# Decoder layer with two token mixers: gate projections by a scheme of seven block products on three of eight weight units, the two branch products moved behind them

## The chip, the core and the metric

The kernel runs on one core of a Trainium2 chip. The metric is the device time of one execution in microseconds (us). Five engines work side by side, each on a queue of its own that it takes in order: TensorE (PE; its weight loads are shown as PEld), VectorE (DVE), ScalarE (ACT), GpSimd (POOL) and SyncE (SP). SP issues the weight transfers from HBM; POOL issues the small transfers inside the layer. An engine that waits for a semaphore holds everything that stands behind it on its own queue.

## The reference, cut to what matters

256 tokens, width 2048, everything in fp32:

```
h = rmsnorm(x);  proj = h @ w_in        # q_a, c_kv, k_rope, z_mla, c_in, b_gate, c_gate, z_conv, g_mla, g_conv
attn  = causal_attention(...) * silu(z_mla);            y_mla  = attn @ w_o_mla
conv  = b_gate * conv3(c_gate * c_in) * silu(z_conv);   y_conv = conv @ w_o_conv
merged = sigmoid(g_mla) * y_mla + sigmoid(g_conv) * y_conv
out = x + rmsnorm(merged @ w_out)
```

The change touches `g_mla` and `g_conv` (two products of 256 x 2048 tokens with 2048 x 2048 weights), `y_mla`, `y_conv` and the order of the four.

## The kernel before

Every fp32 operand is held as two float32r parts: hi (rounded) and lo (the rest, source minus hi). A product of two operands is three matmuls, hi x hi, hi x lo and lo x hi (`product`). Weights come in units of 128 x 2048 fp32 (1 MB): SP loads a unit into one of three `raw` buffers, ACT writes hi (`whi`, L237) and DVE writes lo (`wlo`, L238), in halves of 1024 columns with five half buffers each. `take(i)` asks for unit i, keeps three loads ahead and splits one unit ahead. A plain unit holds four K rows of blocks: 4 K blocks x 2 token tiles x 3 = 24 matmuls of 128 x 512.

The order of the work is written out; PE keeps it. A first part makes the low-rank products, z, attention by heads and four convolution products per column block (`cv`, 16 x 4 units). A column block of the convolution is drained from PSUM by `channels_done` (L695 on ACT, L697 on ACT, L700 on DVE); the two PSUM banks `cv` are then free for the next one. `taps` and `channels_join` finish the convolution; `turned` (L312 to L323) transposes a tile on DVE into a buffer (`via`, `cw` or `mv`), sends it in four POOL transfers to DRAM (`far`) and brings it back in one.

The second part (`tokens`, PSUM tiles `sq`) goes over four blocks c of 512 output columns, and in each over n = g_mla, g_conv, y_mla, y_conv: four units each, 64 units and 1536 matmuls. The two gates read the tokens in `x_both` (hi and lo, 16 K blocks), the branches read `at_both` and `cv_both`, which ACT and DVE split from `at_f` and `cv_f` while the first gates run. A gate's PSUM goes through a sigmoid on ACT into a small buffer (L897); the branch sums are multiplied in on DVE (L907, L912, L913). The merged block is turned and split into `m_both` while the next block's products run. The third part (`out`) multiplies `m_both` by w_out in 16 units and normalises.

Pools are stacked: a pool opened after another has closed takes its memory, so its first writer waits for all readers of what lay there. The large pool `bp` holds the buffers of the first part, among them `cw` and `mv`, from which the last convolution tiles leave by POOL transfers.

Of the kernel before, what the change touches and what calls it, by code (L numbers as in the profile page):

```python
# [23 lines left out]
H = 16  # L24
# [13 lines left out]
UNIT = 2048  # L38
LINE = 32
HALF = UNIT // 2  # L40
SQ = S // 4
XW = S + R


PV = {}
# [34 lines left out]


@with_exitstack
def tile_layer(ctx: ExitStack, tc: tile.TileContext, xw, x, pos, pvec, post_g, wc, wz, wcv, wkr, wqk, wqr, wv, cwr, wsq, out):
    nc = tc.nc

    def matmul(*a, **kw):
# [9 lines left out]
    part = top.tile([P, LINE], F32, name="part")[:, :NT]  # L96
# [3 lines left out]
    wpool = ctx.enter_context(tc.tile_pool(name="wpool", bufs=1))  # L100
# [4 lines left out]

    plan = []

    def add(ap, width=UNIT):
        plan.append((ap, width))
        return len(plan) - 1  # L110


# [8 lines left out]
    for h in range(H):  # L121
        g, second = divmod(h, HG)
# [3 lines left out]
    order = []  # L126
# [11 lines left out]
        else:  # L138
            u_head[i][j] = add(wcv[i, j])

    u_d = [[[add(wsq[n, c, k]) for k in range(4)] for n in range(4)] for c in range(4)]
# [3 lines left out]
    u_out = {ck: add(wsq[4, ck[0], ck[1]]) for ck in out_order}  # L145

    raws, splits, early = {}, {}, {}
    done = {"raw": 0, "split": 0}

    def load_raw(i):  # L150
        ap, w = plan[i]
        t = early.get(i)
        if t is None:
            t = wpool.tile([P, UNIT], F32, name=f"raw{i}", tag="raw", bufs=3)
        cuts = {0: (S, XW, 2 * XW), 1: (0, XW, 2 * XW), 2: (0, XW, 2 * XW)}.get(i, (0, w))
        for a, b in zip(cuts[:-1], cuts[1:]):
            nc.sync.dma_start(out=t[:, a:b], in_=ap[:, a:b])
        raws[i] = t
        if i == u_ckv[1]:
            tc.keep_in_program_order(nc.sync.dma_start(out=x_tok, in_=x))  # L160

    def split_unit(i):
        t, w = raws.pop(i), plan[i][1]
        parts = []
        if i == u_kr:
            t = t[:, :w].rearrange("p (k c) -> p k c", k=KD)
            for h in range(2):
                both = wpool.tile([P, HALF], F32R, name=f"whi{i}_{h}", tag="whi", bufs=5)
                both = both[:, :].rearrange("p (k j c) -> p k j c", k=KD // 2, j=2)
                ks = slice(h * KD // 2, (h + 1) * KD // 2)  # L170
                split_act(both[:, :, 0], both[:, :, 1], t[:, ks])
                parts.append(both.rearrange("p k j c -> p k (j c)"))
            splits[i] = parts
            return
        if i <= u_qa[-1]:

            hi, lo = (wpool.tile([P, HALF], F32R, name=f"{o}{i}", tag=o, bufs=5) for o in ("whi", "wlo"))
# [5 lines left out]
            splits[i] = [(hi, lo)]  # L183
            return
        for h in range(0, w, HALF):
            n = min(HALF, w - h)
            if u_out[3, 0] <= i < u_out[3, 3]:
                hi, lo = (op.tile([P, HALF], F32R, name=f"w{o}{i}_{h}") for o in ("hi", "lo"))
            else:
                hi = wpool.tile([P, HALF], F32R, name=f"whi{i}_{h}", tag="whi", bufs=5)  # L190
                lo = wpool.tile([P, HALF], F32R, name=f"wlo{i}_{h}", tag="wlo", bufs=5)
            split_act(hi[:, :n], lo[:, :n], t[:, h : h + n])
            parts.append((hi, lo))
        splits[i] = parts

    def ahead(i, raw=3, split=1):
        while done["raw"] < min(i + raw, len(plan)):
# [9 lines left out]
    def take(i):  # L207
        ahead(i)
        parts = splits.pop(i)

        def piece(j, n):
            o = j * n
            h, o = o // HALF, o % HALF
            return parts[h][0][:, o : o + n], parts[h][1][:, o : o + n]

        return piece

# [18 lines left out]
    def split_act(hi, lo, src, keep=False):  # L236
        a = nc.scalar.activation(hi, src, AF.Copy)  # L237
        b = nc.vector.tensor_tensor(lo, src, hi.bitcast(F32), op=ALU.subtract)  # L238
        if keep:

            tc.keep_in_program_order(a)
            tc.keep_in_program_order(b)
# [30 lines left out]


    main = ctx.enter_context(ExitStack())
    hp = main.enter_context(tc.tile_pool(name="hp", bufs=1))
# [562 lines left out]


    bstack.close()
    cp = main.enter_context(tc.tile_pool(name="cp", bufs=1))
    at_both = cp.tile([P, H, 2 * S], F32R, name="at_both")
    cv_both = cp.tile([P, KD, 2 * S], F32R, name="cv_both")
    dp = main.enter_context(tc.tile_pool(name="dp", bufs=1))

    def split_turned(src, both, c, t):
        ks, ts = slice(4 * c, 4 * c + 4), slice(t * P, (t + 1) * P)
        lo = slice(t * P + S, (t + 1) * P + S)
        split_act(quarters(both[:, ks, ts]), quarters(both[:, ks, lo]), by_rows(src, 4), True)  # L850

    def split_branch(i):

        for t in range(NT):
            split_turned(at_t[:, i, t, :], at_both, i, t)

    def split_channels(i):

        j, t = divmod(i, NT)
        split_turned(cv_t[:, j, t, :], cv_both, j, t)  # L860

    def tokens(c, n, cols):

        pss = [bank(f"sq{c}_{n}_{t}") for t in range(NT)]
        for kk in range(4):
            w = take(u_d[c][n][kk])
            if c == 0 and n == 0:
                split_branch(kk)
            if c == 0 and n in (1, 2):
                split_channels(4 * (n - 1) + kk)  # L870
# [7 lines left out]
    def wide(name, t, bufs=1):  # L878
        return dp.tile([P, 512], F32, name=f"{name}{t}", tag=f"{name}{t}", bufs=bufs)

    def features(c, m, m_both):

        for t in range(NT):
            split_turned(m[t][:, :], m_both, c, t)

    waiting = m_both = None
    for c in range(4):
        gates = []
        for n in range(2):
            pss = tokens(c, n, x_both)  # L890
            if waiting is not None:
                features(c - 1, waiting, m_both)
                waiting = None
            sg = []
            for t in range(NT):
                g = wide(f"sg{n}_", t)
                nc.scalar.activation(g[:, :], pss[t][:, :], AF.Sigmoid, scale=r_col[:, t : t + 1])  # L897
                sg.append(g)
            gates.append(sg)
        m = gates[0]  # L900
        pss = tokens(c, 2, at_both)
        if c == 0:
            fstack.close()
            merged_pool = ctx.enter_context(tc.tile_pool(name="merged_pool", bufs=1, side="right"))
            m_both = merged_pool.tile([P, KD, 2 * S], F32R, name="m_both")
        for t in range(NT):
            nc.vector.tensor_tensor(m[t][:, :], pss[t][:, :], m[t][:, :], op=ALU.mult)  # L907
        pss = tokens(c, 3, cv_both)
        steps = []
        for t in range(NT):  # L910
            y = gates[1][t]
            nc.vector.tensor_tensor(y[:, :], pss[t][:, :], y[:, :], op=ALU.mult)  # L912
            nc.vector.tensor_tensor(m[t][:, :], m[t][:, :], y[:, :], op=ALU.add)  # L913
            steps.append(turned(m[t][:, :], y[:, :], 4))
        for go, _ in steps:
            go()
        for t, (_, come) in enumerate(steps):
            come(m[t][:, :])
# [36 lines left out]
    last = []  # L955
# [33 lines left out]
        finish(t, out_block(3, t, pss[t]))  # L989


def _cols(w):

    k, n = w.shape
    return np.ascontiguousarray(
        w.reshape(k // P, P, n // P, P).transpose(2, 1, 0, 3)
    ).reshape(n // P, P, k)


def _feat(v):  # L1000
# [79 lines left out]
```

## Time and profile before

| | |
|---|---|
| median of three runs | 1045.03 us (1044.26 to 1047.25) |
| span of the profiled execution, first to last instruction | 1045.6 us |
| second part (`sq`), on PE | starts at 602.63, ends at 950.83 |
| third part (`out`), on PE | ends at 1037.88 |

The span of the profiled execution lies inside the range of the three runs, 0.6 us above their median. A row of the timeline gives the start, the time, the engine, the line, what is written and read, how many instructions, and in brackets how long the engine was idle before it and what ended that. A row of the groups gives the count, the busy time, the mean of one in ns, and the idle time before.

### The profile page before, as it was taken

To read this page: it belongs to the slowest core of one execution; us is meant where nothing else is said; L and a number is where in the kernel's file an instruction comes from. 1 tells how busy PE (TensorE), PEld (TensorE's weight loads), DVE (VectorE), ACT (ScalarE), POOL (GpSimd) and SP (SyncE) were. 2 spreads that over 40 slices of the span, in tenths; PEclk is the share of its full clock that TensorE was granted. 3 is DMA by queue.
4 is the path that set the end of the run, shared out by engine and by line. 5 is a ranking of instruction groups with operands and counts; after the bars stand their busy time and mean duration, and the time that the engine had idled before them with its cause. 6 is when DMAs were issued, how large, how long until landed. Compare 5 with 4: busy or idle time off the path is not lost.

```text
span 1045.6 us, 12715 instructions
## 1 busy us (share of the span) xinstructions
PE 1029.9 (98%) x4694; PEld 857.5 (82%) x4694; DVE 684.0 (65%) x954; ACT 529.5 (51%) x731; POOL 179.7 (17%) x345
## 2 busy tenths in 40 slices
PE   9999999999999999999999999999999999999997
PEld 8888887888878878788888888888888888888885
DVE  7578778686787667777777776555564456445562
ACT  7766556555455455554555455434444434443451
POOL 7611221204111132212222220020010002002000
PEclk9999999999999999999999999999999999999999
DMA  8755766658665685757676865575566556558642
GB/s 344 297 187 189 255 206 207 223 200 306 186 228 214 199 288 174 266 195 243 210 254 218 277 208 201 201 242 189 181 211 225 201 191 223 195 197 318 236 171 81
DMA packets 41951, 231.04 MB, mean 221 GB/s; under 512 B 7520, under 2 KB 8224, under 8 KB 18976
## 3 DMA queue, kind: packets, MB, share of 16 engines
q1 hardware_dynamic: 29808, 197.54, 53.6%
q0 software_dynamic: 11648, 29.38, 8.5%
q10 hardware_dynamic: 432, 3.29, 0.8%
q8 instruction: 37, 0.61, 0.2%
q14 instruction: 26, 0.21, 0.1%
HBM read 214.48 MB, written 11.53 MB: 216 GB/s over the span
## 4 chain that ended last, share of the span: by engine, by line
PE 88%; DMA 4%; DVE 4%; issue 2%; ACT 1%; POOL 1%; DVEq 0%; POOLq 0%; ACTq 0%
PE sq L88 33%; PE cv L88 26%; PE out L88 8%; PE z L88 7%; DMA cw<-cwr_dram 2%; PE qa L88 2%; PE ckv L88 2%; PE vv L88 2%; PE kn L88 2%; PE qn L88 2%; DVE wlo L238 1%; PE sc L88 1%; DMA far<-via 1%; PE o L88 1%; DMA p<-far 1%
## 5 line engine op out<-in xcount | busy, mean ns | idle before, releaser
L238 DVE TENSOR_TENSOR wlo<-raw,whi 128x1024 fp32r<-128x1024 f32 (+1 forms) x370 | 441.8, 1198 | 295.3 <-ACT whi L237 284.8
L237 ACT ACTIVATE whi<-raw 128x1024 fp32r<-128x1024 f32 (+1 forms) x372 | 382.8, 1035 | 413.9 <-PE sq L88 181.1
L88 PE MATMUL cv<-whi,x_both 128*128 128x512 f32 x1024 | 324.6, 391 | 6.5 <-DVE cv_w L700 4.5
L88 PEld LDWEIGHTS cv<-whi,x_both 128*128 128x128 f32 x1024 | 193.0, 189 | 47.0 <-DVE cv_w L700 5.1
L88 PE MATMUL cv<-wlo,x_both 128*128 128x512 f32 x512 | 200.3, 391 | 0.0
L88 PE MATMUL sq<-whi,x_both 128*128 128x512 f32 x512 | 158.4, 389 | 0.0
L88 PEld LDWEIGHTS sq<-whi,x_both 128*128 128x128 f32 x512 | 96.1, 188 | 20.0
L88 PEld LDWEIGHTS cv<-wlo,x_both 128*128 128x128 f32 x512 | 96.6, 189 | 18.9
L88 PE MATMUL sq<-wlo,x_both 128*128 128x512 f32 x256 | 99.6, 389 | 0.0
L88 PE MATMUL z<-whi,x_both 128*128 128x512 f32 x256 | 80.6, 390 | 0.0
L88 PE MATMUL sq<-whi,at_both 128*128 128x512 f32 x256 | 79.5, 389 | 0.0
L88 PE MATMUL sq<-whi,cv_both 128*128 128x512 f32 x256 | 79.5, 389 | 0.0
L88 PE MATMUL out<-whi,m_both 128*128 128x512 f32 x256 | 78.9, 389 | 0.0
L319 POOL DMA_DIRECT2D far<-sg x32 | 17.5, 553 | 314.0 <-DVE sg L312 238.7
L319 POOL DMA_DIRECT2D far<-via x64 | 35.3, 558 | 209.7 <-DVE via L312 209.5
L88 PEld LDWEIGHTS sq<-whi,at_both 128*128 128x128 f32 x256 | 48.0, 188 | 10.0
L88 PEld LDWEIGHTS sq<-whi,cv_both 128*128 128x128 f32 x256 | 48.0, 188 | 10.0
L88 PEld LDWEIGHTS out<-whi,m_both 128*128 128x128 f32 x256 | 48.0, 188 | 9.9
L88 PEld LDWEIGHTS z<-whi,x_both 128*128 128x128 f32 x256 | 48.1, 188 | 9.9
L88 PEld LDWEIGHTS sq<-wlo,x_both 128*128 128x128 f32 x256 | 48.0, 188 | 9.9
L88 PE MATMUL z<-wlo,x_both 128*128 128x512 f32 x128 | 49.8, 389 | 0.0
L88 PE MATMUL sq<-wlo,at_both 128*128 128x512 f32 x128 | 49.8, 389 | 0.0
(212 smaller groups left out, 1129.1 us busy)
## 6 DMA issues: line engine op xcount, KB each, us to landing
raw<-wsq_dram SPq DMA_DIRECT2D x80, 1024.0 KB, 4.7
raw<-wcv_dram SPq DMA_DIRECT2D x64, 1024.0 KB, 5.4
raw<-wz_dram SPq DMA_DIRECT2D x16, 1024.0 KB, 4.8
raw<-wqk_dram SPq DMA_DIRECT2D x8, 1024.0 KB, 5.4
cw<-cwr_dram POOLq DMA_DIRECT2D x24, 256.0 KB, 5.9
raw<-wc_dram SPq DMA_DIRECT2D x4, 1024.0 KB, 10.0
raw<-wv_dram SPq DMA_DIRECT2D x4, 1024.0 KB, 4.8
far<-via POOLq DMA_DIRECT2D x64, 48.0 KB, 3.3
```

What stands on the lines that cost most here:

```text
L88: return tc.keep_in_program_order(nc.tensor.matmul(*a, **kw))
L237: a = nc.scalar.activation(hi, src, AF.Copy)
L238: b = nc.vector.tensor_tensor(lo, src, hi.bitcast(F32), op=ALU.subtract)
L319: tc.keep_in_program_order(nc.gpsimd.dma_start(out=f[i], in_=m))
```

## The change

Gates first. The two gates are no longer computed per column block beside the branches, but all at once, in four blocks (gate n, half b of 1024 columns), each with eight units of 128 x 2048: two K blocks by 1024 columns. In each block three units are a "pair" (K blocks k and k+4 for k = 0, 1, 2), five are "whole" (plain). Pairs and whole units alternate; the first block begins with a whole unit. A whole unit has 8 block products (2 K blocks x 2 token tiles x 2 column halves), 24 matmuls. For a pair, the same 8 block products are got from seven, 21 matmuls, with sums of weight blocks (`split_pair`: three DVE operations on the raw unit and a buffer `tf`, then hi and lo of seven blocks) and sums of token blocks (`token_sums`, once, tile `xs`).

The seven partial sums and the fourth plain corner take all eight PSUM banks (`g`). After the last pair, `p1` and `p5` are copied by ACT and three DVE operations make the shared sums `u`; at a block's end DVE adds them to four banks (L967) and ACT takes the sigmoid, into `sg`, which holds both gates whole in SBUF.

Branches in turn. y_mla is computed for all four column blocks and multiplied into `sg`, then y_conv for all four; features of block c are split after the products of block c+1. `at_both` and `m_both` now are the memory of `x_both`; `cv_both` takes the memory of the gate buffers.

Buffers. `whi` and `wlo` become three buffers of a whole unit in place of five of half a unit. First-part units are still split in two halves (two instructions), second- and third-part units in one instruction of 2048 columns. The scratch for POOL's transfers goes from 16384 to 4096 bytes per partition.

```
-                both = wpool.tile([P, HALF], F32R, name=f"whi{i}_{h}", tag="whi", bufs=5)
+        hi = wpool.tile([P, UNIT], F32R, name=f"whi{i}", tag="whi", bufs=3)
...
+    def split_pair(i, t, hi, lo):
+        raw = t[:, :].rearrange("p (b c) -> p b c", b=4)
+        tf = d1.tile([P, 3, 512], F32, name=f"tf{i}", tag="tf", bufs=1)
+        thi, tlo = (d1.tile([P, 3, 512], F32R, name=f"t{o}{i}", tag=f"t{o}", bufs=1) for o in ("hi", "lo"))
+        tt = nc.vector.tensor_tensor
+        tt(tf[:, :2], raw[:, 1:3], raw[:, 0:1].to_broadcast([P, 2, 512]), op=ALU.subtract)
+        tt(raw[:, 0], raw[:, 2], tf[:, 0], op=ALU.add)
+        tt(tf[:, 2], raw[:, 3], raw[:, 0], op=ALU.subtract)
+        split_act(hi[:, :], lo[:, :], t[:, :])
+        split_act(thi[:, :, :], tlo[:, :, :], tf[:, :, :])
...
     bstack.close()
+    sgp = main.enter_context(tc.tile_pool(name="sgp", bufs=1))
+    sg = sgp.tile([P, 2, NT, D], F32, name="sg")
+    dstack = main.enter_context(ExitStack())
+    d1 = dstack.enter_context(tc.tile_pool(name="d1", bufs=1))
+    at_both = m_both = x_both
...
+    def token_sums():
+        both = x_both[:, :, :].bitcast(F32).rearrange("p (g k) c -> p g k c", k=STEP)[:, :2, :PAIRS]
+        xf = d1.tile([P, 2, PAIRS, S], F32, name="xf", tag="tf", bufs=1)
+        s = d1.tile([P, 4, PAIRS, P], F32, name="xsf", tag="thi", bufs=1)
+        for g in range(2):
+            tt(xf[:, g], both[:, g, :, :S], both[:, g, :, S:], op=ALU.add)
+        ...
+        for i in range(4):
+            split_act(xs[:, i, :, 0], xs[:, i, :, 1], s[:, i])
...
+    TAGS = {7: ("mm", 4), 5: ("mm", 4), 1: ("mm", 4), 6: ("mm", 4), 4: ("cv", 2), 2: ("cv", 2), 3: ("st", 1), 0: ("o", 1)}
...
+            if n == b == i == 0:
+                token_sums()
+            w = take(units[i])
+            if kind == "pair":
+                for m in TAGS:
+                    if m:
+                        add_to(m, side(m, ks[0]), w[m], i, True)
...
+        for m, t, half, other in ((2, 0, 0, p1[:, :]), (3, 0, 1, u[:, 0]), (4, 1, 0, u[:, 2]), (0, 1, 1, u[:, 1])):
+            tt(g, ps[m][:, :], other, op=ALU.add)
+            nc.scalar.activation(g, g, AF.Sigmoid, scale=r_col[:, t : t + 1])
...
     for c in range(4):
+        pss = tokens(c, 0, at_both)
+        for t, m in enumerate(merged(0, c)):
+            nc.vector.tensor_tensor(m, pss[t][:, :], m, op=ALU.mult)
...
+        pss = tokens(c, 1, cv_both)
```

**Order of the instructions, place 1: DVE where the second part begins.** Before (L numbers of the kernel before; the names in brackets are the semaphores that an instruction waits for, DMASW0 to 7 being those of POOL's transfers, DMAHW those of SP's):

```order
L700 SCALAR_TENSOR_TENSOR cv_w<-cv_1_5349,r_both,cv_w 128x512 [waits PE_49]
L312 STREAM_TRANSPOSE mv_5530<-cv_f 128x4x4x32 [waits DVE_49]
L238 TENSOR_TENSOR wlo_0_5591<-raw_5550,whi_0_5590 128x1024 [waits DMAHW0_49,Activation_49]
L386 TENSOR_TENSOR f<-o_5511,half 128x256 [waits Activation_49]
L704 TENSOR_TENSOR cv_f<-cv_f,cv_w 128x512 [waits DVE_49]
L645 TENSOR_TENSOR at_f<-f,at_f 128x8x32 [waits DVE_49]
L312 STREAM_TRANSPOSE cw<-cv_f 128x4x4x32 [waits DVE_49]
L238 TENSOR_TENSOR wlo_1024_5595<-raw_5550,whi_1024_5594 128x1024 [waits Activation_49]
L238 TENSOR_TENSOR wlo_0_5629<-raw_5588,whi_0_5628 128x1024 [waits DMAHW1_49,Activation_49]
```

Now, the same place; `xf` and `xsf` are the token sums, of which `xs` are the parts hi and lo:

```order
L726 SCALAR_TENSOR_TENSOR cv_w<-cv_1_5162,r_both,cv_w 128x512 [waits PE_49]
L338 STREAM_TRANSPOSE mv_5333<-cv_f 128x4x4x32 [waits DVE_49]
L412 TENSOR_TENSOR f<-o_5314,half 128x256 [waits Activation_49]
L730 TENSOR_TENSOR cv_f<-cv_f,cv_w 128x512 [waits DVE_49]
L671 TENSOR_TENSOR at_f<-f,at_f 128x8x32 [waits DVE_49]
L338 STREAM_TRANSPOSE cw<-cv_f 128x4x4x32 [waits DVE_49]
L899 TENSOR_TENSOR xf<-x_both 128x768 [waits DMASW4_49,DMASW3_49,DMASW5_49,DMASW2_49,DMASW6_49,DMASW1_49,DMASW7_49,DMASW0_49,DVE_49]
L899 TENSOR_TENSOR xf<-x_both 128x768
L903 TENSOR_TENSOR xsf<-xf 128x384 [waits DVE_49]
L901 TENSOR_TENSOR xsf<-xf 128x384 [waits DVE_49]
L902 TENSOR_TENSOR xsf<-xsf,xf 128x384 [waits DVE_49]
L264 TENSOR_TENSOR xs<-xsf,xs 128x3x128 [waits Activation_49] x2
```

The weight splits that stood among and behind the last joins are gone from here; in their place DVE stops at the first token sum until POOL's transfers are through. The program's counts say which: six of the eight semaphores must stand at 416 and two at 432, 16 per transfer, and POOL's transfers go round the eight in turn, so 8 x 26 + 2 = 210 of the 212 transfers that stand ahead of the first `far<-sg` must have landed: all but the two that bring `cv_f` back.

The rows of DVE that follow, up to the second pair (`tf` and `raw` are the weight sums, `tlo` is the lo part of `tf`):

```order
L904 TENSOR_TENSOR xsf<-xf,xsf 128x384 [waits DVE_49]
L264 TENSOR_TENSOR xs<-xsf,xs 128x3x128 [waits Activation_49]
L210 TENSOR_TENSOR tf_5379<-raw_5282 128x1024 [waits DMAHW7_49,DVE_49]
L264 TENSOR_TENSOR xs<-xsf,xs 128x3x128 [waits Activation_49]
L211 TENSOR_TENSOR raw_5282<-raw_5282,tf_5379 128x512 [waits DVE_49]
L212 TENSOR_TENSOR tf_5379<-raw_5282 128x512 [waits DVE_49]
L264 TENSOR_TENSOR wlo_5378<-raw_5282,whi_5377 128x2048 [waits Activation_49]
L264 TENSOR_TENSOR wlo_5416<-raw_5375,whi_5415 128x2048 [waits DMAHW0_49,Activation_49]
L264 TENSOR_TENSOR tlo_5381<-tf_5379,thi_5380 128x1536 [waits Activation_49]
```

The lo part of the next whole unit (`wlo_5416`) stands ahead of the lo part of the first pair (`tlo_5381`); ACT's queue has the same order (`whi_5377`, `whi_5415`, `thi_5380`).

**Place 2: PE at the first pair.** Before, the first gate (`sq`) went on from unit to unit. Now the last matmuls of the first whole unit and the first of the pair read:

```order
L90 MATMUL g_0_5358<-whi_5284,x_both 128x512 [waits DVE_49]
L90 MATMUL g_0_5358<-wlo_5285,x_both 128x512
L90 MATMUL g_0_5358<-whi_5284,x_both 128x512 x2
L90 MATMUL g_0_5358<-wlo_5285,x_both 128x512
L90 MATMUL g_0_5358<-whi_5284,x_both 128x512
L90 MATMUL g_7_5351<-thi_5380,xs 128x512 [waits DMASW3_49,DMASW4_49,DMASW2_49,DMASW5_49,DMASW1_49,DMASW6_49,DMASW0_49,DMASW7_49,Activation_49,Pool_49]
L90 MATMUL g_7_5351<-tlo_5381,xs 128x512 [waits DVE_49]
L90 MATMUL g_7_5351<-thi_5380,xs 128x512
```

One whole unit stands ahead of the pair; the pair's second matmul needs the last of the DVE rows above.

**Place 3: ACT inside the first part, ahead of a drain of `cv`.** Before, the two halves of a unit wait for PE one after the other:

```order
L237 ACTIVATE whi_0_1616<-raw_1581 128x1024 [waits DMAHW7_49,PE_49,Activation_49]
L237 ACTIVATE whi_1024_1620<-raw_1581 128x1024 [waits PE_49,Activation_49]
L385 ACTIVATE half<-o_1565 128x256 [waits PE_49]
L237 ACTIVATE whi_0_1651<-raw_1614 128x1024 [waits DMAHW0_49,PE_49,Activation_49]
L237 ACTIVATE whi_1024_1655<-raw_1614 128x1024 [waits DVE_49,PE_49]
```

Now they wait once, for a whole buffer, and follow each other:

```order
L263 ACTIVATE whi_1571<-raw_1536 128x1024 [waits DMAHW7_49,PE_49,Activation_49]
L263 ACTIVATE whi_1571<-raw_1536 128x1024
L411 ACTIVATE half<-o_1520 128x256 [waits PE_49,Activation_49]
L263 ACTIVATE whi_1604<-raw_1569 128x1024 [waits DMAHW0_49,PE_49,Activation_49]
L263 ACTIVATE whi_1604<-raw_1569 128x1024
```

The wait that the second half had is now ahead of the first. In the program the first half of `whi34` waited for PE's count 697 and the second for 703; the whole unit now waits for 703.

More of the change, by code (lines that the diff above doesn't have):

```diff
@@ L106, in tile_layer, with add @@
     plan = []
-    def add(ap, width=UNIT):
-        plan.append((ap, width))
+    def add(ap, width=UNIT, kind="half"):
+        plan.append((ap, width, kind))
         return len(plan) - 1
@@ L175, in split_unit @@
         if i <= u_qa[-1]:
-            hi, lo = (wpool.tile([P, HALF], F32R, name=f"{o}{i}", tag=o, bufs=5) for o in ("whi", "wlo"))
+            hi, lo = slot(i)
             for j in range(2):
@@ L182, in split_unit @@
                 split_act(hi[:, j * R : (j + 1) * R], lo[:, j * R : (j + 1) * R], t[:, o + S : o + XW], True)
-            splits[i] = [(hi, lo)]
+            splits[i] = hi, lo
             return
[L185 to L194, printed above, removed]
+        if u_out[3, 0] <= i < u_out[3, 3]:
+            hi, lo = (op.tile([P, UNIT], F32R, name=f"w{o}{i}") for o in ("hi", "lo"))
+        else:
+            hi, lo = slot(i)
+        if kind == "pair":
+            splits[i] = split_pair(i, t, hi, lo)
+            return
+        n = HALF if kind == "half" else UNIT
+        for h in range(0, w, n):
+            e = min(h + n, w)
+            split_act(hi[:, h:e], lo[:, h:e], t[:, h:e])
+        splits[i] = hi, lo
+    def split_pair(i, t, hi, lo):
[8 more added lines that the diff above has]
+        split_act(thi[:, :, :], tlo[:, :, :], tf[:, :, :])
+        w = {}
+        for n, b in ((6, 0), (1, 1), (3, 2), (2, 3)):
+            w[n] = [a[:, b * 512 : (b + 1) * 512] for a in (hi, lo)]
+        for n, b in ((5, 0), (7, 1), (4, 2)):
+            w[n] = [a[:, b] for a in (thi, tlo)]
+        return w
     def ahead(i, raw=3, split=1):
@@ L209, in take @@
         parts = splits.pop(i)
+        if isinstance(parts, dict):
+            return parts
         def piece(j, n):
-            o = j * n
-            h, o = o // HALF, o % HALF
-            return parts[h][0][:, o : o + n], parts[h][1][:, o : o + n]
+            return tuple(a[:, j * n : (j + 1) * n] for a in parts)
         return piece
@@ new lines, in side, with wide @@
+    def side(n, j):
+        i = {5: 0, 6: 1, 7: 2, 3: 3}.get(n)
+        if i is not None:
+            return [xs[:, i, j, h] for h in range(2)]
+        k, t = {1: (j, 0), 2: (j + STEP, 0), 4: (j + STEP, 1)}[n]
+        return [x_both[:, k, o + t * P : o + (t + 1) * P] for o in (0, S)]
+    def wide(name):
+        return d1.tile([P, 512], F32, name=name, tag=name, bufs=1)
+    TAGS = {7: ("mm", 4), 5: ("mm", 4), 1: ("mm", 4), 6: ("mm", 4), 4: ("cv", 2), 2: ("cv", 2), 3: ("st", 1), 0: ("o", 1)}
@@ L862, in tokens @@
+    for n in range(2):
+        for b in range(2):
+            gate_block(n, b, n == b == 1)
+    split_branch(3)
+    dstack.close()
+    cvp = main.enter_context(tc.tile_pool(name="cvp", bufs=1))
+    cv_both = cvp.tile([P, KD, 2 * S], F32R, name="cv_both")
     def tokens(c, n, cols):
@@ L865, in tokens @@
         for kk in range(4):
[L866 to L870, printed above, removed]
+            w = take(u_d[n][c][kk])
+            if n == 0 and c < 2:
+                split_channels(4 * c + kk)
             for t in range(NT):
@@ L989, in tile_layer, with gate_kinds @@
         finish(t, out_block(3, t, pss[t]))
+def gate_kinds():
+    pairs = [("pair", (k, k + STEP)) for k in range(PAIRS)]
+    paired = {k for _, ks in pairs for k in ks}
+    rest = [k for k in range(KD) if k not in paired]
+    plain = [("whole", ks) for ks in zip(rest[::2], rest[1::2])]
+    alternate = []
+    for i, pair in enumerate(pairs):
+        alternate += [pair, plain[i]]
+    alternate += plain[PAIRS:]
+    late = [plain[-1]] + [u for u in alternate if u != plain[-1]]
+    return {(n, b): late if n == b == 0 else alternate for n in range(2) for b in range(2)}
 def _cols(w):
@@ L997, in _cols, with _gate_unit @@
     ).reshape(n // P, P, k)
+def _gate_unit(w, kind, ks):
+    a, b = (w[k] for k in ks)
+    order = ((a, 1), (a, 0), (b, 1), (b, 0)) if kind == "pair" else ((a, 0), (a, 1), (b, 0), (b, 1))
+    return np.concatenate([m[:, half] for m, half in order], axis=1)
 def _feat(v):
@@ L1063 @@
             w.reshape(4, 4, P, 4, 512).transpose(3, 0, 2, 1, 4).reshape(4, 4, P, UNIT)
[L1064 removed]
+            for w in (w_o_mla, w_o_conv, w_out)
         ]),
+        "wg": np.stack([
+            np.stack([_gate_unit(w.reshape(KD, P, 2, 2, 512)[:, :, b], *u) for u in kinds[n, b]])
+            for n, w in enumerate((g_m, g_c)) for b in range(2)
+        ]).reshape(2, 2, KD // 2, P, UNIT),
     }
[L1068 removed]
+    nc = bacc.Bacc("TRN2", target_bir_lowering=False, num_devices=1, dynamic_dma_scratch_size=4096)
     ins, args = {}, []
```

121 lines of the change are left out of this document (73 added, 48 removed).

## Prediction

> **What bounds the kernel now.** I read first the page's busy times, then the chain that ended last in order of time, then the busy time of the second part alone.
>
> ```profile
> PE 1029.9 (98%) x4694; PEld 857.5 (82%) x4694; DVE 684.0 (65%) x954; ACT 529.5 (51%) x731; POOL 179.7 (17%) x345
> ...
> 602.06 0.57 PE o L88 x4
> 602.63 348.20 PE sq L88 x1536
> 950.83 87.05 PE out L88 x384
> ...
> 602.63:950.83 348.20, 348.20 (x1537) 288.29 (x1537) 191.02 (x186) 155.84 (x167) 22.14 (x41) 1.00 0.59 205
> ```
>
> PE is the bound. In the second part the chain is one piece of PE without a gap: 348.20 us for 1536 matmuls, 0.2267 us each. DVE is busy 191 of these 348 us, ACT 156, so what they do there is hidden as long as it comes in time. Each matmul less is worth 0.2267 us, and each us in which PE finds an operand missing costs a full us.
>
> **What is removed.** 12 pair units lose one product of three matmuls each: 36 matmuls, 36 x 0.2267 = **-8.2 us**. The order of PE's instructions bears this out (732 matmuls for the gates in place of 768).
>
> **What is added on DVE and ACT.** The rows that price it:
>
> ```profile
> L238 DVE TENSOR_TENSOR wlo<-raw,whi 128x1024 fp32r<-128x1024 f32 x352 | 429.5, 1224 | 295.3 <-ACT whi L237 284.8
> L237 ACT ACTIVATE whi<-raw 128x1024 fp32r<-128x1024 f32 x352 | 370.8, 1059 | 412.2 <-PE sq L88 181.1 <-PE cv L88 137.6 <-PE z L88 33.0
> L351 ACT ACTIVATE cv_f<-cv_f 128x2048 f32<-128x2048 f32 x2 | 3.8, 1900 | 0.0
> L238 DVE TENSOR_TENSOR pt<-p,pt 128x384 fp32r<-128x384 f32 x16 | 8.8, 549 | 2.1 <-ACT pt L237 2.1
> L238 DVE TENSOR_TENSOR cv_both<-cv_f,cv_both 128x512 fp32r<-128x512 f32 x8 | 5.5, 683 | 0.0
> L907 DVE TENSOR_TENSOR sg<-sq,sg 128x512 f32<-128x512 f32 x8 | 5.5, 687 | 1.2 <-PE sq L88 1.2
> ...
> 621.26 4.90 DVE L238 TENSOR_TENSOR at_both<-at_f,at_both 128x512 fp32r<-128x512 f32 x8
> ```
>
> On DVE 384, 512 and 1024 columns take 0.549, 0.683 and 1.224 us, 0.135 per 128 columns. No row has 768, 1536 or 2048 columns; by this line they take 0.95, 1.76 and 2.30 (bounds: no better than the line without its constant, 2.16 for 2048; no worse than pieces of 512, 2.73). Eight pieces of 512 in a row took 4.90, so each costs its successor only 0.61: 0.07 to 0.09 less than its mean. ACT takes 1.06 for 1024 and 1.90 for 2048, so 1.48 for 1536. Reading from PSUM costs the same (0.687).
>
> A pair and the whole unit behind it cost DVE 1.14 + 0.6 + 0.7 (sums) + 2.2 + 1.7 + 2.2 (lo parts) = 8.5 us; PE takes 45 x 0.2267 = 10.2 for them. Over a block it is 34.7 of 41.5 with the sums `u` and the four closing additions. ACT has less. By the bound with pieces of 512 DVE needs 10.2 and 41.6, just PE's time. So in the middle of the gates I take **0** (bounds 0 and 6); the cover is PE's 10.2 us. At a block's end PE returns to the bank `g_4` only after 12 matmuls (2.7 us) of the next pair, and that bank was full 1.36 us before the end: 4 us for two or three additions of 0.6 and one lo part of 2.2 on DVE; I take 0. Loads stay 1 MB a unit:
>
> ```profile
> raw<-wsq_dram SPq DMA_DIRECT2D x80, 1024.0 KB, 4.7
> ```
>
> 4.7 us to landing, three ahead: hidden under 4.8 to 5.4 us of PE per unit. Longer splits for the branches and w_out are fewer instructions on engines that wait for PE anyway: 0. The branches themselves are moved, not changed.
>
> **Where a wait is added: the first pair.** The end of the first part on DVE and POOL:
>
> ```profile
> 602.39 1.22 DVE L238 TENSOR_TENSOR wlo<-raw,whi 128x1024 fp32r<-128x1024 f32 x1
> 603.53 0.74 DVE L700 SCALAR_TENSOR_TENSOR cv_w<-cv,r_both,cv_w 128x512 f32<-128x512 f32 x1
> 604.19 0.70 DVE L312 STREAM_TRANSPOSE mv<-cv_f 128x512 f32<-128x512 f32 x1
> 604.81 1.18 DVE L238 TENSOR_TENSOR wlo<-raw,whi 128x1024 fp32r<-128x1024 f32 x1
> 605.92 0.41 DVE L386 TENSOR_TENSOR f<-o,half 128x256 f32<-128x256 f32 x1
> 606.25 0.68 DVE L704 TENSOR_TENSOR cv_f<-cv_f,cv_w 128x512 f32<-128x512 f32 x1
> 606.85 0.42 DVE L645 TENSOR_TENSOR at_f<-f,at_f 128x256 f32<-128x256 f32 x1
> 607.18 0.70 DVE L312 STREAM_TRANSPOSE cw<-cv_f 128x512 f32<-128x512 f32 x1
> ...
> 608.18 2.21 POOL L319 DMA_DIRECT2D far<-cw  x4 [13.04 <-DVE cw L312]
> 610.38 2.17 POOL L319 DMA_DIRECT2D far<-mv  x4
> 615.85 1.21 POOL L323 DMA_DIRECT2D cv_f<-far  x2 [3.31 <-DMA far<-mv]
> ...
> DMA to landing us min/median/max: 1.9/4.8/5.8
> ```
>
> Before, DVE went on with weight splits at 607.88 and nobody waited for the transposed tiles. Now the next instruction on DVE is the first token sum, and it may not start until the eight transfers out of `cw` and `mv` have landed. Behind it stand, in DVE's order, all that the first pair needs. Step by step, on the clock of before:
>
> - The last transposition ended at 607.88. Two weight splits of 1.14 are gone from ahead of it: 605.6.
> - From there to the landing of the last transfer it took 615.85 - 607.88 = 8.0 us (4.4 of it POOL's eight issues): 613.6. Bounds from the landing times: the last issue began 4.1 after the transposition, so 6.0 to 9.9.
> - Token sums and the first weight sums on DVE until the raw unit is ready: 2 x 0.87 + 8 x 0.47 + 1.14 + 0.7 = 7.4: 621.0.
> - ACT makes the pair's hi part, 1.9, while DVE stands; then DVE makes its lo part (2.2), the lo part of the next whole unit, which the order puts first (2.2), and the pair's `tlo` (1.8): 629.1. ACT keeps up: its second and third part (1.8, 1.5) end by 626.3.
> - PE starts the gates at 602.63, has one whole unit, 24 x 0.2267 = 5.44, and one matmul of the pair: it stops at 608.3 and resumes at 629.1.
>
> That is a stall of **+20.8 us** (18.8 to 22.7 by the landing, 1.3 more by the long pieces). PE cannot go round it, since it takes its queue in order, and the gates behind the pair are behind the stall. Nothing of it is won back, because PE was and is the bound behind it.
>
> **The restart.**
>
> ```profile
> 1038.00:1045.60 7.60, 0.00 (x0) 0.00 (x0) 3.63 (x7) 0.89 (x3) 0.00 (x0) 0.79 0.37 138
> ...
> 1.13 4.02 PE L88 MATMUL idle<-ones 128*128 128x128 f32 x18 [1.13 <-POOL hpi L261]
> ...
> 52.28 0.60 PE L88 MATMUL rb<-dg,ones 128*128 128x128 f32 x4
> 52.64 0.48 PE L88 MATMUL z<-whi,x_both 128*128 128x512 f32 x1
> 4.91 0.47 PE L88 MATMUL qa<-whi,x_both 128*128 128x512 f32 x1
> ```
>
> In the last 7.6 us, where PE has nothing to do, the granted clock is 0.79. And at the kernel's start 18 records of the small fp32 form took 4.91 - 1.13 = 3.78 us, 0.21 each, where four of the same form later took 0.36, 0.09 each: coming from rest, PE lost 3.78 - 18 x 0.09 = 2.2 us. A stall of 20 us is a rest of that kind: **+2.0** (0 to 2.2).
>
> [...]
>
> **The first part.** Its PE order is the same, but its buffers are not.
>
> ```profile
> PE cv L88 <- DVE cv_w L700: 4.5, 3, 2.4
> PE cv L88 <- ACT cv_f L695: 2.0, 1, 2.0
> ...
> 153.12 1.06 ACT L237 ACTIVATE whi<-raw 128x1024 fp32r<-128x1024 f32 x1 [3.03 <-PE cv L88]
> 154.49 1.06 ACT L237 ACTIVATE whi<-raw 128x1024 fp32r<-128x1024 f32 x1 [0.31 <-PE cv L88]
> 163.55 0.69 DVE L733 TENSOR_TENSOR cv_f<-cv_f,cw 128x512 f32<-128x512 f32 x1 [0.74 <-DMA cw<-cwr_dram]
> 166.66 1.71 DVE L452 TENSOR_TENSOR rp_b<-f,sin_t 32x256 f32<-32x256 f32 x4
> 168.40 0.75 DVE L700 SCALAR_TENSOR_TENSOR cv_w<-cv,r_both,cv_w 128x512 f32<-128x512 f32 x1
> 169.21 0.50 PE L88 MATMUL cv<-whi,x_both 128*128 128x512 f32 x1 [0.97 <-DVE cv_w L700]
> ```
>
> Four times a drain of `cv` holds PE, 6.5 us in all. Now the first half of a unit waits for the later release, so the two halves end 2 x 0.96 after it in place of 1.06, about 0.9 later, and DVE, POOL's `cw` load and the drain (`cv_w`) behind them too. Against this the order drops the rope pieces (1.7) ahead of the drain and adds one lo half (1.14): 0.5 to 0.6 earlier. Net 0.4 at each of three places: **+1.2**. Bounds: all these waits vanish (-6.5), or each of the four is as long as the longest (4 x 2.4 - 6.5 = +3.1). I stay near the row worked out.
>
> **Sum.** -8.2 + 20.8 + 2.0 + 1.2 = **+15.8** on the span of 1045.6 gives 1061.4. That span is 0.6 above the median of the runs, so 1045.0 + 15.8, rounded to **1061 us**.
>
> **Rivals.**
>
> - *The first pair comes in time.* For it: in the second part DVE and ACT are idle for 157 and 192 of 348 us. Then only the matmuls count: 1045.0 - 8.2 + 1.2 = 1038. It decides at one place, the pair's second matmul: with restart and first part as above the change wins if `tlo` is ready within 5 us of PE's stop at 608.3, by 613.3, when by the rows the token sums have not begun. Against it stands DVE's order. Faster: 4%.
> - *The drain costs nothing, only the chain of sums does* (the counted transfers have landed by the time of the transposition): sums from 605.6 on, `tlo` at 621.1, stall 12.8, time 1053. Against: transfers cannot leave before their transposition, and 8.0 us were seen. 6%.
> - *DVE becomes the bound in the gates as well.* If the long pieces cost like pieces of 512, DVE meets PE's time with nothing spare, and each late closing addition holds the next block's banks: +6, time 1067, up to 1070. For: three single buffers (`tf`, `thi`, `tlo`) tie pairs together. 14%.
> - That the matmuls do not fall by 36 is excluded by the order.
>
> **Chances and range.** The forecast (1056 to 1066) has 74%, the rivals 4, 6 and 14; 2% are left for a result near no change, in which a stall of about 5 us eats the gain. The range must take in the landing's bounds (2 either way), restart (-2), the first part (-6.5 to +2, most of it unlikely) and the third rival: **1053 to 1071**. About 0.3% is what a measurement here can tell from no change. Faster by more than that 0.04, within it 0.02, slower 0.94.
>
> **What would show it.** One idle stretch of PE of about 21 us before the first `g` matmul with `tlo`, put down to DVE; DVE idle for about 8 us before the first `xf`, ended by a transfer out of `mv` or `cw`; PE without gaps through the rest of the gates and the branches; 36 matmuls less; waits of `cv` for `cv_w` of 5 to 8 us in all. I am wrong if PE's idle time at the first pair is under 10 us, or if the gaps are spread over the pairs.

## The result, and the profile after

| | before | after |
|---|---|---|
| median of four runs each | 1045.72 us (1044.26 to 1047.25) | 1059.04 us (1057.66 to 1061.09) |
| ratio after / before, 95% interval | | 1.0115 (1.008 to 1.0151) |
| profiled execution: time, span | 1047.25 us, span 1045.6 us | 1061.09 us, span 1059.3 us |

The change makes the kernel slower by 13.3 us by the medians and by 13.7 us from span to span; 1061 with 1053 to 1071 had been forecast. One correction to what was said of the time before: an execution lasts 1.7 to 1.8 us longer than its span (1061.09 against 1059.3 after the change), so the span of 1045.6 belongs to the slowest run of the kernel before, at 1047.25, and not to one 0.6 above the median. The sum of the forecast was 1061.4 for the span, and 1059.3 was measured. The differences from trace to trace below are not touched by that. One of the 23 runs of the kernel before that stand beside `e1` to `e4` below was slow (1058.33 us); without it their median is 1045.45 in place of 1045.62, which shifts each difference from it by 0.2 us.

The busy times and the granted clock on the page of the kernel after:

```profile
PE 1024.0 (97%) x4658; PEld 851.8 (80%) x4658; DVE 742.5 (70%) x960; ACT 532.5 (50%) x675; POOL 180.3 (17%) x345
...
PEclk9999999999999999999999969999999999999999
```

PE has 36 instructions fewer (4694 to 4658) and is busy 5.9 us less, yet the span is longer: it waits, at one place, where the clock row has its single 6. The end of the chain in order of time, and the longest waits of PE (us in total, times, longest):

```profile
628.14 162.30 PE g L90 x707
790.44 174.08 PE sq L90 x768
964.52 87.05 PE out L90 x384
...
PE g L90 <- ACT thi L263: 16.5, 1, 16.5
PE cv L90 <- DVE cv_w L726: 3.3, 4, 1.1
PE o L90 <- DVE pt L264: 2.6, 1, 2.6
PE g L90 <- DVE tlo L264: 2.2, 1, 2.2
PE sc L90 <- DVE qr L264: 1.7, 1, 1.7
```

From 628.14 to the end PE runs without a gap, with 707 of the 732 gate matmuls in the first piece. The other 25 lie ahead of it, and the two large `g` waits are one stall at the first pair. PE's own rows there:

```profile
603.00 0.39 PE L90 MATMUL g<-whi,x_both 128*128 128x512 f32 x1
...
608.25 0.39 PE L90 MATMUL g<-whi,x_both 128*128 128x512 f32 x1
625.17 0.77 PE L90 MATMUL g<-thi,xs 128*128 128x512 f32 x1 [16.53 <-ACT thi L263]
628.14 0.79 PE L90 MATMUL g<-tlo,xs 128*128 128x512 f32 x1 [2.21 <-DVE tlo L264]
```

By the pitch of 0.2267 us the pair's second matmul, the first with `tlo`, was due at 608.25 + 2 x 0.2267 = 608.70. It starts at 628.14: 19.4 us late. What DVE did meanwhile:

```profile
605.24 0.70 DVE L338 STREAM_TRANSPOSE cw<-cv_f 128x512 f32<-128x512 f32 x1
612.52 1.82 DVE L899 TENSOR_TENSOR xf<-x_both 128x768 f32<-128x768 f32 x2 [6.57 <-DMA far<-mv]
...
619.27 0.68 DVE L211 TENSOR_TENSOR raw<-raw,tf 128x512 f32<-128x512 f32 x1
...
621.93 4.49 DVE L264 TENSOR_TENSOR wlo<-raw,whi 128x2048 fp32r<-128x2048 f32 x2 [1.25 <-ACT whi L263]
626.34 1.75 DVE L264 TENSOR_TENSOR tlo<-tf,thi 128x1536 fp32r<-128x1536 f32 x1
```

DVE itself stands for 6.57 us behind the last transposition, until POOL's last transfer out of `mv` has landed. Then come the token sums, the weight sums, ACT's hi part, and on DVE two lo parts of 2048 columns ahead of the `tlo` that PE wants. The stretches of the second part and the branches (busy time of PE, PEld, DVE, ACT and POOL, then granted clock, DMA share and GB/s):

```profile
608.50:632.00 23.50, 4.76 (x11) 3.36 (x11) 16.86 (x19) 8.90 (x8) 3.55 (x7) 0.56 0.39 128
632.00:790.40 158.40, 158.40 (x700) 131.13 (x699) 135.00 (x105) 88.33 (x70) 0.00 (x0) 1.00 0.57 199
790.40:964.50 174.10, 174.10 (x770) 144.16 (x769) 100.39 (x77) 71.08 (x51) 16.43 (x30) 1.00 0.61 212
```

In the first, PE works 4.76 of 23.50 us at a clock of 0.56. In the other two it never stops. DVE is busy 85% of the rest of the gates, and that costs nothing.

### The profile page after: what moved, and what is told of

The parts are those of the page before. It is cut to its first block, busy times and chain, and to the rows that moved or that the text cites. A ratio compares the mean times of both kernels' runs of the same rounds, so it can differ in the third digit from the quotient of the medians.

```text
span 1059.3 us, 12469 instructions
## 1 busy us (share of the span) xinstructions
PE 1024.0 (97%) x4658; PEld 851.8 (80%) x4658; DVE 742.5 (70%) x960; ACT 532.5 (50%) x675; POOL 180.3 (17%) x345
## 4 chain that ended last, share of the span: by engine, by line
PE 90%; DVE 4%; issue 2%; DMA 2%; ACT 1%; POOL 1%; DVEq 0%; POOLq 0%
PE cv L90 28%; PE sq L90 16%; PE g L90 15%; PE z L90 8%; PE out L90 8%; PE qa L90 2%; PE qn L90 2%; PE ckv L90 2%; PE kn L90 2%; DMA cw<-cwr_dram 2%; PE vv L90 2%; PE sc L90 1%; DVE wlo L264 1%; ACT whi L263 1%; PE o L90 1%
## 5 line engine op out<-in xcount | busy, mean ns | idle before, releaser
L264 DVE TENSOR_TENSOR wlo<-raw,whi 128x1024 fp32r<-128x1024 f32 (+2 forms) x290 | 423.4, 1484 | 224.7 <-ACT whi L263 223.8
L263 ACT ACTIVATE whi<-raw 128x1024 fp32r<-128x1024 f32 (+2 forms) x292 | 357.5, 1259 | 380.3 <-issue 120.5
L90 PE MATMUL g<-whi,x_both 128*128 128x512 f32 x368 | 119.8, 390 | 0.0
L90 PEld LDWEIGHTS cv<-wlo,x_both 128*128 128x128 f32 x512 | 96.2, 188 | 18.7
L90 PEld LDWEIGHTS g<-whi,x_both 128*128 128x128 f32 x368 | 69.4, 189 | 14.4
L90 PE MATMUL sq<-whi,x_both 128*128 128x512 f32 x256 | 79.0, 389 | 0.0
L90 PE MATMUL out<-whi,x_both 128*128 128x512 f32 x256 | 78.9, 389 | 0.0
L90 PE MATMUL g<-wlo,x_both 128*128 128x512 f32 x184 | 71.8, 390 | 0.0
L90 PEld LDWEIGHTS sq<-whi,x_both 128*128 128x128 f32 x256 | 48.0, 188 | 9.9
L90 PE MATMUL sq<-wlo,x_both 128*128 128x512 f32 x128 | 49.8, 389 | 0.0
L90 PE MATMUL sq<-wlo,cv_both 128*128 128x512 f32 x128 | 49.8, 389 | 0.0
```

The source lines that it names most:

```text
L90: return tc.keep_in_program_order(nc.tensor.matmul(*a, **kw))
```

## The experiments

The theory: the loss is a single stall at the first pair. DVE must first wait for the convolution's last transfers to leave their buffers, and only then works off the chain that ends with the first `tlo`; a short restart at half clock (0.50 granted from 628.20 to 631.70) comes on top. The rivals: the new order and buffers cost the time; the pairs load DVE too heavily all through the gates; the pair waits for something other than DVE's chain. Each number below is a median of the runs of its kernel, beside runs of the kernel before on the same chip: 1045.62 us for `e1` to `e4`, 1045.79 us for `e5`, `e6`, `e7` and `e4b`.

### e1: all units plain

```
+    alternate = [("whole", (k, k + 1)) for k in range(0, KD, 2)]
+    late = alternate
-            if n == b == i == 0:
+            if n == b == 0 and i == 99:        # token_sums() is never called
```

> The change with plain units alone: gates first, the new buffers, the branches in turn, all 1536 matmuls, no pairs, no token sums; nothing of the computation is left out. If the loss sits at the first pair, there is no stall at the start of the gates and the time is that of the kernel before, plus 0 to 1.5 us (first part +0.4 in the change's trace). If the reordering or the buffers cost the time, it stays about 13 us above the kernel before.

Measured: 1047.48 us, ratio 1.0014 (0.9996 to 1.0033). The stall is gone, and the gates first, the branches in turn and the new buffers cost 1.9 us together by the medians (-0.4 to 3.5 us by the interval; 0 to 1.5 was expected). So this part of the change is not where 13 us went. The trace has one small thing of its own, in a row of PE and in a stretch of PE (length, busy time, granted clock, DMA share, GB/s):

```profile
601.36 0.55 PE L90 MATMUL o<-pt,vv_hi 128*128 128x512 f32 x1 [2.26 <-DVE pt L264]
...
601.90:605.10 3.20, 3.20 (x11) 0.51 0.07 23
```

After a rest of 2.26 us PE gets half the clock (0.51) for 3.2 us, and the 768 gate matmuls take 175.35 us where 768 x 0.2267 is 174.1. These 1.2 us are as much as the whole difference of the two spans, 1046.8 against 1045.6. In the changed kernel the same instruction came after 2.61 us of rest (the `pt` wait above), and the gates began at full pace (1.00 granted from 602.80 to 608.40).

### e2: first block plain, pairs in the other three

```
+    order = "WWWWWWWW"                        # W whole, P pair; first block only
+            if n == b == 0 and i == 4:        # token_sums()
```

> The first of the four gate blocks holds eight plain units, the token sums are made under it, and pairs stand in the other three blocks. 27 matmuls fewer than before. If the loss is one stall at the first pair: no idle stretch of PE at the start of the gates, time 6.1 us below the kernel before plus 0.4, so 5 to 6 us faster than before. If pairs overload DVE all along the gates, three blocks with nine pairs keep three quarters of the loss: some 8 to 10 us slower than before, with gaps at the pairs.

Measured: 1041.74 us, ratio 0.9964 (0.9949 to 0.9979): faster than the kernel before, with nine of the twelve pairs kept. All gates are one piece of the chain:

```profile
601.62 168.24 PE g L90 x741
```

741 x 0.2267 = 168.0: no gap. Pairs as such do not overload DVE, and the rival of a load all through the gates falls. Against the plain order (1047.48) it wins 5.7 us, near the 27 x 0.2267 = 6.1 us that the missing matmuls are worth; against the kernel before it is 3.9, short of the 5 to 6 expected, as the plain order itself lies 1.9 us behind by the medians.

### e3: the last tiles leave from buffers of their own

```
+    jp = fstack.enter_context(tc.tile_pool(name="jp", bufs=1, side="right"))
+        if j == 3:
+            via = jp.tile([P, 512], F32, name=f"join{t}")
```

> The change with one thing taken away: the last two convolution tiles leave from two buffers in a pool of their own, so that the token sums need not wait for POOL's transfers. If this drain is on the path: the first token sum starts right behind the last transposition, 6.6 us earlier, PE's stall falls from 19.4 to about 13 us, time about 6.7 us above the kernel before. If the chain of sums alone sets the end (the drain is hidden under something else): time as the change, 13 us above before.

Measured: 1053.02 us, ratio 1.0074 (1.0053 to 1.0095), 7.4 us above the kernel before where the changed kernel is 13.3 above it. DVE and PE:

```profile
604.41 0.70 DVE L339 STREAM_TRANSPOSE join<-cv_f 128x512 f32<-128x512 f32 x1
605.04 1.79 DVE L903 TENSOR_TENSOR xf<-x_both 128x768 f32<-128x768 f32 x2
...
617.65 0.77 PE L90 MATMUL g<-thi,xs 128*128 128x512 f32 x1 [9.84 <-issue]
620.62 0.80 PE L90 MATMUL g<-tlo,xs 128*128 128x512 f32 x1 [2.21 <-DVE tlo L264]
```

The token sums follow the transposition without a pause, and PE waits 12.1 us in place of 18.7: 6.7 less, about the 6.57 us for which DVE had stood; by the medians it is 5.9 less. The wait for the transfers is shown to be a full part of the loss; the rest of the stall is DVE's chain.

### e5: the pair's lo part ahead of the next unit's

```
-        split_act(thi[:, :, :], tlo[:, :, :], tf[:, :, :])
+        split_act(thi[:, :, :], tlo[:, :, :], tf[:, :, :], True)   # True: keeps program order on ACT and DVE
+            split_act(hi[:, h:e], lo[:, h:e], t[:, h:e], kind == "whole" and i <= u_g[0][3])
```

> The four-million-product order is untouched; only VectorE's order within the first units of the gates is the program's, so that the pair's residual tlo (1.75 us) stands ahead of the next whole unit's wlo (2.29 us). Theory (the stall is VectorE's chain of work between the landed convolution product and tlo): tlo ends about 2.3 us earlier, TensorE resumes near 625.9 instead of 628.1, and the time is 2 to 2.5 us below the changed kernel's, about 1056.7. Rival (the pair waits for something else, its raw part's arrival or ScalarE's share of the split, and the wait on tlo only comes last): resumption within 0.5 us of 628.1 and a time equal to the changed kernel's, 1059.

Measured: 1058.72 us, ratio 1.0111 (1.0079 to 1.0143), 12.9 us above the kernel before. The expected gain of 2 to 2.5 us is not in the time. DVE's and PE's rows:

```profile
604.17 0.70 DVE L338 STREAM_TRANSPOSE cw<-cv_f 128x512 f32<-128x512 f32 x1
611.42 1.83 DVE L899 TENSOR_TENSOR xf<-x_both 128x768 f32<-128x768 f32 x2 [6.56 <-DMA far<-mv]
...
620.83 2.29 DVE L264 TENSOR_TENSOR wlo<-raw,whi 128x2048 fp32r<-128x2048 f32 x1 [1.25 <-ACT whi L263]
623.04 1.75 DVE L264 TENSOR_TENSOR tlo<-tf,thi 128x1536 fp32r<-128x1536 f32 x1
...
601.27 0.47 PE L90 MATMUL g<-whi,x_both 128*128 128x512 f32 x1 [1.43 <-DVE cv_w L726]
...
624.84 0.80 PE L90 MATMUL g<-tlo,xs 128*128 128x512 f32 x1 [1.81 <-DVE tlo L264]
```

From the last transposition to the first `tlo` matmul it takes 624.84 - 604.17 = 20.7 us, in the changed kernel 628.14 - 605.24 = 22.9: the chain is 2.2 shorter, as a lo part less in it should make it, so `tlo` on DVE is what PE waits for. The edit moves ACT's `thi` ahead of the next unit's `whi` as well. In the old order `thi` would have ended near 624.0, an estimate from ACT's 1.9 and 1.5 us for the two in this trace, and `tlo` could not have begun at 623.04; so the 2.2 us belong to both moves together. But fixing the order moved other instructions too. The transposition now comes 2.9 us after the gates' first matmul in place of 2.2, and a later pair, at 673.80, waits 0.6 us for its `tlo`. That leaves 2.2 - 0.7 - 0.6 = 0.9 us where the medians show 0.3, and two medians of a few runs can differ by as much: in the traces of kernels with the same first part the gates begin at 600.47 (`e4`), 601.54 (`e4b`) and 603.00 (the changed kernel). The reading of the chain holds; the expectation that only its length would move did not.

### e4 and e4b: needless matmuls in the stall

```
+            if n == b == i == 0:
+                for _ in range(70):           # 82 in the second kernel
+                    matmul(ps[7][:, :], x_both[:, 0, :P], x_both[:, 0, :], start=True, stop=True)
```

The results of these matmuls are thrown away; they only keep PE at work. With 70 of them:

> The change with 70 needless matmuls (15.9 us) put on PE into a bank that the first pair then starts afresh, so that PE is not at rest during the stall; the stall's end is set by DVE as before. If the restart at a lower clock costs 1.8 us: time 1.8 us less than the change (about 11.5 above the kernel before), and the matmuls behind the stall come at 0.227 us. If the slow matmuls behind the stall are due to something else (operands that come late): no gain, about 13 us above before.

Measured: 1058.16 us, ratio 1.0128 (1.0102 to 1.0154). PE's rows:

```profile
605.93 16.03 PE L90 MATMUL g<-x_both 128*128 128x512 f32 x70
622.63 0.47 PE L90 MATMUL g<-thi,xs 128*128 128x512 f32 x1 [0.67 <-issue]
625.60 0.68 PE L90 MATMUL g<-tlo,xs 128*128 128x512 f32 x1 [2.50 <-DVE tlo L264]
```

The filler ended 3 us too early, and with one matmul in 3.6 us PE fell to half pace all the same (the seven matmuls from 626.08 took 2.98 us, 0.43 each in place of 0.2267). That settled nothing, so it was made longer. With 82:

> 82 needless matmuls of 128x128 by 128x512 on TensorE behind the first whole unit, whose results are discarded, so that it works through nearly all of the stall (606.6 to about 625.4, 82 x 0.2267 = 18.6 us). Theory (the matmuls behind the stall come at half pace because TensorE had rested): with no rest over 1 us left the eight matmuls at 0.427 us each run at 0.2267, and the time is 1.6 to 2 us below the changed kernel's, about 1057.3; if the filler outlasts the wait by x us, x more. Rival (the half pace has another cause, such as VectorE's and ScalarE's load at that place): the matmuls after tlo come at 0.42 us as before, and the time is that of the changed kernel or above.

Measured: 1056.95 us, ratio 1.0094 (1.0062 to 1.0127), 2.1 us below the changed kernel, 11.2 above the kernel before. PE's rows, two stretches of PE, and the chain's next piece:

```profile
625.61 0.39 PE L90 MATMUL g<-thi,xs 128*128 128x512 f32 x1
626.67 0.50 PE L90 MATMUL g<-tlo,xs 128*128 128x512 f32 x1 [0.67 <-DVE tlo L264]
...
606.80:625.60 18.80, 18.80 (x84) 1.00 0.28 78
626.70:630.20 3.50, 3.50 (x15) 1.00 0.77 318
...
626.67 160.59 PE g L90 x707
```

The stretch behind the stall in the changed kernel, for comparison:

```profile
628.20:631.70 3.50, 3.50 (x8) 0.50 0.79 309
```

With the filler PE works through the stall and comes out of it at full clock, 15 matmuls in 3.5 us and not 8: the same 707 matmuls take 160.59 us in place of 162.30. The half clock after the stall is thus PE's own rest and costs 1.7 us. It is not DVE's load, which is the same in both (busy 2.53 and 2.56 of the 3.5 us). The rest of the stall is untouched, since `tlo` comes no earlier.

### e6 and e7: pairs late in the first block

Two kernels with the order `WWWWPWPW` in the first block (two pairs there, eleven in all). One has the buffers of their own from above and the token sums at unit 1:

```
+    order = "WWWWPWPW"
+            if n == b == 0 and i == 1:        # token_sums(); with jp as above
```

> First block in the order whole, whole, whole, whole, pair, whole, pair, whole (two pairs, eleven in all, 33 matmuls fewer than before), token sums one unit later, and the last two joins of the convolution leave from buffers of their own. Theory: the first pair is wanted four units (96 matmuls, 21.8 us) after the gates begin, near 624, and the sums start near 605 and take about 12 us with the pair's split, so there is no stall and all of 33 x 0.2267 = 7.5 us shows, less 0 to 2 us at the start of the gates: 1038 to 1040.5, ratio 0.993 to 0.995. Rival (pairs cost VectorE more than TensorE gives it, so that a stall of some size comes wherever the first pair stands): at least 5 us of TensorE waiting in the gates and a time of 1043 or more.

Measured: 1041.45 us, ratio 0.9958 (0.9938 to 0.9978), 4.3 us below the kernel before. DVE's and PE's rows:

```profile
606.42 1.82 DVE L903 TENSOR_TENSOR xf<-x_both 128x768 f32<-128x768 f32 x2
...
619.61 1.75 DVE L264 TENSOR_TENSOR tlo<-tf,thi 128x1536 fp32r<-128x1536 f32 x1
...
624.04 0.39 PE L90 MATMUL g<-tlo,xs 128*128 128x512 f32 x1
...
648.89 0.50 PE L90 MATMUL g<-whi,x_both 128*128 128x512 f32 x1 [1.11 <-DVE sg L974]
```

`tlo` ends at 621.4, 2.7 us before PE wants it. What is left is a wait of 1.1 us just behind the first block, for an addition that closes it: with a pair next to last the shared sums come late, and the next block's pair wants all eight banks. That is argued and was not tried apart; it is about the 1 us by which the time lies above the 1038 to 1040.5 expected. The other kernel shares the convolution's buffers as the changed kernel does, with the sums at unit 2:

> The same order of units as the kernel with late pairs and own buffers, the token sums two units later, but the convolution's buffers are shared as in the changed kernel, so the sums cannot start before the drain has landed, near 612.5. Theory: from 612.5 the sums, the pair's parts and its split take some 13.5 us on VectorE (as from 612.5 to 626.3 in the changed kernel, without the wlo of the unit between: 2.3 less), so tlo is ready at 624 to 626, against 624.3 at which TensorE has done its four whole units: a stall of 0 to 3 us, with up to 2 us of slow clock behind it, and 1038.5 to 1043. Rival (the order alone is no cure, the shared buffers hold the whole chain): a stall of 8 us or more as in the changed kernel and a time above 1046.

Measured: 1048.99 us, ratio 1.0022 (1.0002 to 1.0042): a miss. The time is that of the rival (above 1046), though the stall is near the 0 to 3 us of the theory and far from the rival's 8. ACT's row, DVE's, PE's, and two stretches of PE:

```profile
608.91 1.92 ACT L263 ACTIVATE whi<-raw 128x2048 fp32r<-128x2048 f32 x1 [6.71 <-PE g L90]
...
610.86 2.29 DVE L264 TENSOR_TENSOR wlo<-raw,whi 128x2048 fp32r<-128x2048 f32 x1 [4.66 <-ACT whi L263]
613.07 1.82 DVE L899 TENSOR_TENSOR xf<-x_both 128x768 f32<-128x768 f32 x2
...
622.53 4.49 DVE L264 TENSOR_TENSOR wlo<-raw,whi 128x2048 fp32r<-128x2048 f32 x2 [1.31 <-ACT whi L263]
626.94 1.75 DVE L264 TENSOR_TENSOR tlo<-tf,thi 128x1536 fp32r<-128x1536 f32 x1
...
628.75 0.50 PE L90 MATMUL g<-tlo,xs 128*128 128x512 f32 x1 [2.51 <-DVE tlo L264]
...
602.10:605.60 3.50, 3.50 (x10) 0.53 0.30 37
628.75:632.90 4.15, 4.15 (x12) 0.61 0.67 268
```

The stall at the first pair shrank to 3.5 us (`tlo` was due at 625.25), so the place of the first pair is shown to matter by itself. But the sums, put behind a plain unit's lo part in DVE's order, now wait for that part, which waits for ACT, which waits for PE to release one of three `whi` buffers. And the lo part of the next unit still stands ahead of `tlo` (4.49 for two), 2.2 us that the expectation had left out. PE got a lower clock twice, first at the gates' start (0.53 for 3.5 us) and again after the stall (0.61 for 4.15 us), and a later pair, at 664.01, waited 1.9 us. The theory had allowed for the slow clock after the stall, but not for the one at the start, nor for the later pair. Late pairs need early sums, and early sums need the buffers of their own.

Of all versions the plain first block (1041.74) and the late pairs with own buffers (1041.45) beat both kernels; their intervals do not tell them apart.

## Why the prediction was right, step by step

| step | forecast | measured |
|---|---|---|
| 36 matmuls less | -8.2 | -8.2 (counted: 732 for the gates, 0.2267 each) |
| stall at the first pair | +20.8 | +19.4 |
| restart | +2.0 | +1.7 to +1.8 |
| first part | +1.2 | +0.5 |
| middle and ends of the gates | 0 | 0 |
| sum on the span | +15.8 | +13.7 (0.2 to 0.3 of it not assigned) |

The three terms that were off were all put too high, by 1.4, some 0.3 and 0.7 us, so the forecast did not come near by errors that cancelled; it lies 2.0 us above the median after.

- **Fewer matmuls.** The count and the time of one matmul are as forecast, and the gain is visible only with the stall away: `e2` wins 5.7 us against the plain order for 27 matmuls.
- **The stall.** The mechanism, the place and the order of the steps were as forecast, and `e2`, `e3` and `e5` each took one of them away. The mis-sized term is the drain, put at 8.0 us between transposition and landing; it took 6.6. POOL's issues last as long as before (605.94 to 610.94, 5.0 us, against 4.7); the last transfer was through 1.6 us after the issues ended, where the row of before had 3.3. What the prediction overlooked is what else was moving: before, SP's weight loads took 1.84 of the 2.36 MB moved from 606 to 616 and POOL's transfers out of `cw` and `mv` landed after 4.3 and 4.5 us (medians); in the changed kernel no weight load moved from 604 to 613, and they landed after 1.9. That the weight loads slowed them is argued, not tried apart. From the landing on the chain ran as worked out: raw unit ready 7.4 us later, hi part 1.9, lo parts 2.2, 2.2 and 1.8. The estimates of 2.30 and 1.76 us for 2048 and 1536 columns on DVE measured 2.29 and 1.75.
- **The restart.** 1.7 us by `e4b`, against 2.0 read off the kernel's start. In the changed kernel 0.50 was granted for the 3.5 us from 628.20 to 631.70; half of that, 1.75 us, is an estimate of the loss that agrees with it.
- **The first part.** The first gate matmul starts at 603.00 in place of 602.47 (the 602.63 of the prediction is where the chain's piece begins, at the end of the matmul before). That is 0.5 us, and no more than scatter, since with the same first part it starts at 600.47 in `e4` and at 601.54 in `e4b`. The waits for `cv_w` and `cv_f` fell from 6.5 to 3.3 us and did not grow; two new ones, 2.6 for `pt` and 1.7 for `qr`, took their place. So waits for `cv_w` of 5 to 8 us, named as a sign, did not come; the reason given for this term was wrong, and that its size was near was luck.
- **The rivals.** "The first pair comes in time" is what `e2` and `e6` bring about, and they end below the kernel before, with nine and eleven pairs at 1041.7 and 1041.5, not at 1038. "The drain costs nothing" would have given 1053; `e3` makes it true and gives 1053.02. "DVE becomes the bound in the gates" did not happen: 85% busy, no gap.

## What to carry to other kernels

When a change saves work on the engine that is the bound but feeds it through a longer chain elsewhere, price the first use by itself: here a chain of 22.9 us met a cover of one unit, 5.4 us, and the stall with its restart, 21 us, is more than twice what 36 matmuls saved. Look up which buffers the first instruction of a new stage reuses, and who still has to read them; a pool that closes hands on its readers' waits, transfers included (here 6.57 us). Then try to start with the plain form of the work until the chain has been run through, or give the last readers memory of their own.

## What the hardware showed that was not expected

- In two traces PE's clock fell to half after a short rest. The same instruction at the end of the first part came after rests of 2.26 us (`e1`) and 2.00 us (`e7`), and the granted clock fell to 0.51 and 0.53 for 3.2 to 3.5 us. That cost 1.2 us in `e1` (175.35 - 174.1) and some 1.6 in `e7` (its first 96 matmuls took 23.4 us in place of 21.8); after 2.61 (the changed kernel), 2.56 (`e3`), 2.34 (`e6`) and 2.00 (`e2`) it stayed at 1. So it is not the length of the rest alone. Why the two rests of 2.00 us ended differently was not tried.
- The kernel before varies more from run to run than the versions with the gates first: 1041.29 to 1052.45 us in 22 runs, against 1040.50 to 1043.48 in 12 of `e6`; and 1041.39 to 1052.30 in 22 others, beside 1046.61 to 1048.79 in 12 of `e1`. Part of it goes with the granted clock: the three runs above 1051 have 0.994 to 0.995, the six below 1043 have 0.997 to 0.999. Why was not tried.
